# Moving the last mLSTM head ahead of the last attention pair, and splitting the branch sums into eight parts beside the gate units

## The chip, the cores and the metric

The kernel runs on one core of a Trainium2 chip. A core has five engines that run in parallel, each through its own instruction stream in a fixed order: TensorE (PE, matrix products), VectorE (DVE), ScalarE (ACT), GpSimd (POOL) and SyncE (SP, which here issues nearly all DMAs). An instruction that waits holds up everything behind it on its engine. The metric is the device time of one execution, in microseconds (us); lower is better.

## The reference

One decoder layer on x of 1024 tokens by 1024 channels, in float32. A combined projection feeds two branches: a 4-head mLSTM and a dilated attention with three head groups, whose outputs are summed with weights from their softmax denominators. Both are gated and merged; a SwiGLU block follows. Cut to what matters here:

```python
h    = rmsnorm(x, norm_mix_g)
proj = h @ w_in                       # q,k,v,i,f,o of the mLSTM; q,k,v of attention; two gates
hm   = mlstm_cell(q_m, k_m, v_m, ig, lf)             # 4 heads, chunk by chunk
y_a  = sigmoid(o_pre) * groupnorm(hm)
for g in range(3):                                   # dilations 1, 4, 16
    o_g, lse_g = dilated_window_attention(q_a[g], k_a[g], v_a[g], ...)
wts  = softmax(stack(lses), axis=0)                  # weight of each group, per token and head
y_b  = sum(wts[..., None] * stack(outs), axis=0)     # the sums this change moves
merged = sigmoid(g_A) * (y_a @ w_proj_a) + sigmoid(g_B) * (y_b @ w_proj_b)
x    = x + merged @ w_out
x    = x + (silu(hf @ w_gate) * (hf @ w_up)) @ w_down     # hf = rmsnorm(x)
out  = rmsnorm(x, norm_final_g)
```

## The kernel before

Every product is made in three matmuls on split operands (high and low parts, `whi`/`wlo` for weights), accumulated in PSUM. The projections of 256 columns (a "unit") go through `gemm_s`: a scheme of seven block products of 12 matmuls each (P1, P7, P6, P5, P2, P4, P3; 84 matmuls of 128x512 in all), with three PSUM banks of tag `mm`. ACT copies a first bank out (`u`), DVE adds bank and copy (line 299), and four evacuations follow. For a gate unit an evacuation is the DVE add of line 735, a tanh on ACT, and a store to `gt_d`. A unit's weights come as two raw pieces (tag `raw`, 128x4x256, two buffers), are combined on DVE (lines 244 to 247) and split on ACT and POOL (lines 106, 107).

The steps of the middle of the kernel stand in the string `ORDER`: `mH` is mLSTM head H (two units for q and k, the unit of its output gate, then `mlstm_core`, a chain of small steps), `aGP` an attention pair (two units, then `attn_core`), `rG` moves the maxima and denominators of group G to rows in DRAM (`ml_d`), `c` is `attn_combine`, which makes the group weights and stores them in `c_d` (line 703), `gN` is gate unit N (0 to 3 and 8 to 11; 4 to 7 are the output gates inside the heads), and `sI` the sums of output rows I. A sum multiplies each group's numerators (`num_d`) by its weights, broadcast from `c_d` over 64 partitions by two half loads, and adds the three products (lines 718 and 720); the result is stored in `yb_d`. One 128x512 piece of it needs three pairs of tiles of tag `c`, of which there are six buffers, shared with `mlstm_core`, `attn_core` and the loads behind. `merge_b` (from line 1033 on) loads `yb_d`, splits it into tiles of tag `t`, and multiplies by `w_proj_b` (lines 187 to 189). It needs all of `yb_d` for each of its outputs.

The order within each engine is not the order of the code: a scheduler places instructions by their modelled readiness, with code order as priority and some steps raised by `tc.high_priority()`. Buffers are given out in code order. What results on each engine is fixed before the kernel runs.

Of the kernel before, what the change touches and what calls it, by code (L numbers as in the profile page):

```python
# [14 lines left out]
ALU = mybir.AluOpType  # L15
# [4 lines left out]
P = 128  # L20
S = 1024
# [19 lines left out]
def layer_kernel(ctx, tc, x, norm_mix_g, w_in, b_gate_if, conv_w, conv_b, mlstm_norm_g,  # L41
# [3 lines left out]
    ACT, DVE, POOL, PE, SP = nc.scalar, nc.vector, nc.gpsimd, nc.tensor, nc.sync  # L45
# [10 lines left out]
    def T(tag, shape, dt=F32):  # L56
        cnt[0] += 1
        return sb.tile(list(shape), dt, tag=tag, bufs=SBT[tag], name=f"{tag}{cnt[0]}")
# [223 lines left out]
    def gemm_s(src, c0, B, evac, bk=("mm",) * 4, u1=None):  # L282

        front = u1 is not None
        ops = w7(src, c0, ("A11", "A12") if front else ())
        ba, bc, u2, u3 = PS(bk[0]), PS(bk[1]), T("u", (P, 512)), T("u", (P, 512))
        if not front:
            run_s(ops, "P1", B, ba, True)
            u1 = T("u", (P, 512))
            with tc.high_priority():  # L290
                ACT.activation(u1, ba, AF.Copy)
        run_s(ops, "P7", B, bc, True)
        run_s(ops, "P6", B, ba, front)
        with tc.high_priority():
            if front:
                DVE.tensor_tensor(u2, u1, ba, op=ALU.add)
            else:
                ACT.activation(u2, ba, AF.Copy)  # L298
            DVE.tensor_tensor(u3, u2, bc, op=ALU.add)  # L299
        bd = PS(bk[2])  # L300
        run_s(ops, "P5", B, bd, True)
        evac(1, 1, bd, u3)
        if not front:
            bx = PS(bk[3])
            run_s(ops, "P2", B, bx, True)
            evac(0, 0, bx, u1)
        run_s(ops, "P4", B, bc, False)
        evac(1, 0, bc, u2)
        run_s(ops, "P3", B, bd, False)
        evac(0, 1, bd, u2)  # L310
# [64 lines left out]
    nums_d = [[dr.tile([P, S], F32, name=f"num_d{g}{i}", tag=f"num_d{g}{i}") for i in range(4)] for g in range(3)]  # L375
# [328 lines left out]

    yb_d = [dr.tile([P, S], F32, name=f"yb_d{i}", tag=f"yb_d{i}") for i in range(4)]

    def attn_sum(i):
        for n in range(2):
            sl = slice(n * 512, (n + 1) * 512)
            acc = None  # L710
            for g in range(3):
                cb, nu = T("c", (P, 512)), T("c", (P, 512))
                base = c_d[g, 2 * i]
                for a in range(2):
                    SP.dma_start(cb[a * 64:(a + 1) * 64, :],
                                 bass.AP(tensor=base.tensor, offset=base.offset + a * S + n * 512, ap=[[0, 64], [1, 512]]))
                SP.dma_start(nu, nums_d[g][i][:, sl])
                DVE.tensor_tensor(nu, cb, nu, op=ALU.mult)
                if g:
                    DVE.tensor_tensor(acc, acc, nu, op=ALU.add)  # L720
                else:
                    acc = nu
            SP.dma_start(yb_d[i][:, sl], acc)


    gt_d = dr.tile([24, P, S], F32, name="gt_d", tag="gt_d")
# [4 lines left out]
    def gate_evac(i0):  # L731
        def ev(m, n, p, add):
            t_ = T("e", (P, 512))
            with tc.high_priority():
                DVE.tensor_tensor(t_, p, add, op=ALU.add)
                ACT.activation(t_, t_, AF.Tanh, scale=0.5)
                SP.dma_start(gt_d[i0 + m, :, n * 512:(n + 1) * 512], t_)
        return ev

    def load_gate(tag, i, n):  # L740
        t_ = T(tag, (P, 512))
        SP.dma_start(t_, gt_d[i, :, n * 512:(n + 1) * 512])
        return t_
# [235 lines left out]
        ACT.activation(hi, t1s[k], AF.Copy)  # L979
        DVE.tensor_tensor(lo, t1s[k], f(hi), op=ALU.subtract)  # L980

    ORDER = "m0 a00 a01 r0 m1 a10 a11 r1 m2 a20 a21 r2 c m3 g0 s0 g1 s1 g2 s2 g3 s3 g8 g9 g10 g11".split()
    mlstm_gates()
    mlstm_v2(0)
    for g in range(3):
# [1 line left out]
    bias_rows()  # L987


    def gate_unit(i):  # L990
        i0, c0 = gate_units[i]
        gemm_s(w_in, c0, Bq, gate_evac(i0))

    nm, ll = ([C(f"{n_}{g}", (P, NT, 8)) for g in range(3)] for n_ in ("nm", "ll"))

# [6 lines left out]
    def mlstm_head(h):  # L1002
# [2 lines left out]
        gate_unit(4 + h)  # L1005
        mlstm_core(h, qd, kd)

    for step in ORDER:
        if step[0] == "a":
            attn_pair(int(step[1]), int(step[2]))  # L1010
        elif step[0] == "r":
            attn_rows(int(step[1]), nm[int(step[1])], ll[int(step[1])])
        elif step[0] == "m":
            mlstm_head(int(step[1]))
        elif step[0] == "c":
            attn_combine()
        elif step[0] == "s":
            attn_sum(int(step[1]))
        else:
            gate_unit(int(step[1:]))  # L1020


    mB_d = dr.tile([KD, P, S], F32, name="mB_d", tag="mB_d")
# [10 lines left out]
    def merge_b():  # L1034
        ybs = load_split(yb_d, "t")
        qa = forms_a()
        for u in range(4):
            def ev_z(m, n, p):
                t_ = load_gate("s" if m == 0 else "pt", G_B + 2 * u + m, n)
                DVE.scalar_tensor_tensor(t_, t_, 1.0, p, op0=ALU.add, op1=ALU.mult)  # L1040
                SP.dma_start(mB_d[2 * u + m, :, n * 512:(n + 1) * 512], t_)
            gemm_w(w_proj_b, 0, 4, u * 256, ybs, ev_z)
        return qa
# [96 lines left out]
    for half in range(2):  # L1140
        ts = range(4 * half, 4 * half + 4)
        for u in range(4):
            def ev(t, p):
                sl = slice(u * 256, (u + 1) * 256)
                DVE.scalar_tensor_tensor(acc[t][:, sl], p, 0.5, acc[t][:, sl], op0=ALU.mult, op1=ALU.add)
# [293 lines left out]
```

## Time and profile before

| | us |
|---|---|
| three runs: median (lowest to highest) | 2104.31 (2101.97 to 2121.0) |
| the profiled execution | 2114.06 |
| its span, first to last instruction | 2112.3 |
| TensorE busy within the span | 2016.4 (95%) |
| DVE, POOL, ACT busy | 1316.4, 958.0, 804.4 |

Times within the profile are counted from the start of the span. The mean granted TensorE clock is 0.981 of full speed. The profiled execution is 9.8 us above the median, so a change in it is carried over to the median as a difference.

### The profile page before, as it was taken

Reading aid. Unit: us, or ns where it says so; the run is one execution under the profiler, and the core shown is the slowest. Engines: PE = TensorE matmul, PEld = TensorE weight load, DVE = VectorE, ACT = ScalarE, POOL = GpSimd, SP = SyncE. Lnnn points to the kernel's source line nnn. Section 1 sums busy time; section 2 is a strip of 40 time slices with the busy share of each in tenths; the row PEclk is TensorE's granted clock in tenths of the full one; section 3 lists DMA queues with packets and bytes.
Section 4 is the critical chain, followed back from the end, with each engine's and each line's share of the span. In section 5 each row is a group of like instructions: output and inputs, shape, how many; then the busy total and the mean of one; then the engine's idle time right before and its main releaser. Section 6 shows DMA issues by size and latency. Waiting matters only on the chain.

```text
span 2112.3 us, 31530 instructions
## 1 busy us (share of the span) xinstructions
PE 2016.4 (95%) x11433; PEld 1686.7 (80%) x11433; DVE 1316.4 (62%) x2341; ACT 804.4 (38%) x1722; POOL 958.0 (45%) x723
## 2 busy tenths in 40 slices
PE   6999998999999999999988899999999999999998
PEld 6999877877777677777876677997788888889996
DVE  7832347666786677667757584437755645576776
ACT  5322243343443344345433332445233333344422
POOL 4444443321332224333434656455554555568870
PEclk9999999999999999999999899999999999999999
DMA  4243344433344435555459876753433333375422
GB/s 154 83 120 111 83 133 124 129 127 128 119 130 140 129 123 141 130 183 150 135 168 282 267 233 215 248 181 120 130 96 99 110 95 100 117 247 158 146 83 80
DMA packets 264486, 303.49 MB, mean 144 GB/s; under 512 B 51353, under 2 KB 187052, under 8 KB 264332
## 3 DMA queue, kind: packets, MB, share of 16 engines
q1 hardware_dynamic: 263036, 299.26, 45.8%
q10 hardware_dynamic: 1296, 2.23, 0.3%
q8 instruction: 90, 1.47, 0.3%
q14 instruction: 64, 0.52, 0.1%
HBM read 207.35 MB, written 94.08 MB: 143 GB/s over the span
## 4 chain that ended last, share of the span: by engine, by line
PE 48%; DMA 9%; DVE 8%; POOL 3%; issue 2%; ACT 2%; SPq 1%; DVEq 0%; POOLq 0%; ACTq 0%
PE pmm L268 7%; PE pmm L267 7%; PE pmm L266 7%; DMA c<-num_d 2%; PE pS L268 2%; PE pS L267 2%; PE pS L266 2%; DMA raw<-in_w_in 2%; POOL wlo L107 2%; PE pmm L210 1%; PE pmm L209 1%; PE pmm L211 1%; PE pmm L1314 1%; PE pmm L1315 1%; PE pS L562 1%
## 5 line engine op out<-in xcount | busy, mean ns | idle before, releaser
L107 POOL TENSOR_TENSOR wlo<-sm,whi 128x512 fp32r<-128x512 f32 (+1 forms) x260 | 366.1, 1419 | 512.7 <-ACT whi L106 478.3
L107 POOL TENSOR_TENSOR wlo<-raw,whi 128x512 fp32r<-128x512 f32 (+3 forms) x228 | 339.5, 1502 | 393.5 <-ACT whi L106 376.2
L266 PE MATMUL pmm<-h,whi 128*128 128x512 f32 x824 | 334.1, 405 | 16.8 <-ACT u L298 13.2
L268 PE MATMUL pmm<-h,wlo 128*128 128x512 f32 x824 | 332.1, 403 | 3.8 <-POOL wlo L107 3.8
L267 PE MATMUL pmm<-h,whi 128*128 128x512 f32 x824 | 331.7, 403 | 0.0
L106 ACT ACTIVATE whi<-sm 128x512 fp32r<-128x512 f32 (+1 forms) x260 | 158.8, 634 | 263.2 <-PE pmm L267 128.5
L106 ACT ACTIVATE whi<-raw 128x512 fp32r<-128x512 f32 (+3 forms) x228 | 146.4, 669 | 217.9 <-issue 62.3
L266 PE MATMUL pmm<-t,whi 128*128 128x512 f32 x504 | 204.9, 407 | 13.6 <-DVE u L299 10.5
L266 PEld LDWEIGHTS pmm<-h,whi 128*128 128x128 f32 x824 | 158.5, 192 | 62.4 <-ACT u L298 16.6
L268 PE MATMUL pmm<-t,wlo 128*128 128x512 f32 x504 | 204.0, 405 | 0.0
L267 PE MATMUL pmm<-t,whi 128*128 128x512 f32 x504 | 204.0, 405 | 0.0
L268 PEld LDWEIGHTS pmm<-h,wlo 128*128 128x128 f32 x824 | 157.1, 191 | 41.6 <-POOL wlo L107 4.9
L267 PEld LDWEIGHTS pmm<-h,whi 128*128 128x128 f32 x824 | 157.4, 191 | 38.3 <-issue 3.6
L244 DVE TENSOR_TENSOR sm<-raw,raw 128x512 f32<-128x512 f32 x58 | 44.9, 774 | 181.0 <-DMA raw<-in_w_gate 61.7
L266 PEld LDWEIGHTS pmm<-t,whi 128*128 128x128 f32 x504 | 97.3, 193 | 39.1 <-DVE u L299 12.7
L849 DVE SCALAR_TENSOR_TENSOR c<-c,pm__329,c 128x256 f32<-128x256 f32 x192 | 111.3, 624 | 20.8 <-ACT c L847 20.0
L268 PEld LDWEIGHTS pmm<-t,wlo 128*128 128x128 f32 x504 | 96.7, 192 | 22.9 <-issue 2.2
L267 PEld LDWEIGHTS pmm<-t,whi 128*128 128x128 f32 x504 | 96.6, 192 | 22.3 <-issue 1.5
L589 ACT ACTIVATE s<-s,nm 128x256 f32<-128x256 f32 (+1 forms) x128 | 59.6, 467 | 83.8 <-DVE nm L584 52.3
L209 PE MATMUL pmm<-whi,h 128*128 128x256 f32 (+1 forms) x224 | 64.7, 295 | 5.2 <-DVE ifp L398 4.3
L211 PE MATMUL pmm<-whi,h 128*128 128x256 f32 (+1 forms) x224 | 64.1, 297 | 5.4 <-DVE h L163 3.3
L298 ACT ACTIVATE u<-pmm 128x512 f32<-128x512 f32 x54 | 31.9, 590 | 91.7 <-PE pmm L268 91.7
(549 smaller groups left out, 5065.9 us busy)
## 6 DMA issues: line engine op xcount, KB each, us to landing
raw<-in_w_in SPq DMA_DIRECT2D x74, 512.0 KB
gt_d<-e SPq DMA_DIRECT2D x48, 256.0 KB
raw<-in_w_gate SPq DMA_DIRECT2D x24, 512.0 KB
raw<-in_w_up SPq DMA_DIRECT2D x24, 512.0 KB
raw<-in_w_out SPq DMA_DIRECT2D x16, 512.0 KB
va_d<-u SPq DMA_DIRECT2D x24, 256.0 KB
s<-gt_d SPq DMA_DIRECT2D x24, 256.0 KB
qa_d<-e SPq DMA_DIRECT2D x24, 256.0 KB
```

The source lines that it names most:

```text
L106: ACT.activation(dh, src, AF.Copy)
L107: POOL.tensor_tensor(dl, src, f(dh), op=ALU.subtract)
L209: PE.matmul(p, sh, wh, start=(k == 0), stop=False)
L210: PE.matmul(p, sh, wl, start=False, stop=False)
L211: PE.matmul(p, sl, wh, start=False, stop=(k == K - 1))
L244: DVE.tensor_tensor(s1, a21, a22, op=ALU.add)
L266: PE.matmul(bank, wh[:, k, :], bh, start=start and k == 0, stop=False, skip_group_check=True)
L267: PE.matmul(bank, wh[:, k, :], bl, start=False, stop=False, skip_group_check=True)
L268: PE.matmul(bank, wl[:, k, :], bh, start=False, stop=k == 3, skip_group_check=True)
L298: ACT.activation(u2, ba, AF.Copy)
L589: ACT.activation(s[:, o:o + w], s[:, o:o + w], AF.Exp, bias=nm[:, qt, c:c + 1], accum_out=ll[:, qt, c:c + 1])
L849: DVE.scalar_tensor_tensor(y[:, m, :], xr[:, m, j:j + 256], cw[:, kt, j:j + 1], y[:, m, :], op0=ALU.mult, op1=ALU.add)
```

## The change

`ORDER` puts `m3` (the last mLSTM head) between the units of the attention pairs `a20` and `a21`, so that the pair `a21` is now the last step before `r2` and `c`. The steps `s0` to `s3` go; their work is cut into eight parts (output rows i, token half n), which are attached to the gate units g1 (1 part), g2 (1), g3 (2), g8 (2) and g9 (2). `gate_unit` issues the loads of its first part ahead of its products; after every second evacuation it emits the part's multiplies and adds behind that evacuation on DVE (`tc.issue_after`), and then the loads of the next part. Besides, `merge_b` now writes the four gate loads of a unit ahead of the unit's products instead of in each evacuation.

```diff
+    def sum_load(i, n):
+        sl, tiles = slice(n * 512, (n + 1) * 512), []
+        for g in range(3):
+            cb, nu = T("c", (P, 512)), T("c", (P, 512))
+            base = c_d[g, 2 * i]
+            for a in range(2):
+                SP.dma_start(cb[a * 64:(a + 1) * 64, :],
+                             bass.AP(tensor=base.tensor, offset=base.offset + a * S + n * 512, ap=[[0, 64], [1, 512]]))
+            SP.dma_start(nu, nums_d[g][i][:, sl])
+            tiles.append((cb, nu))
+        return tiles
+
+    def sum_add(i, n, tiles):
+        acc = tiles[0][1]
+        for g, (cb, nu) in enumerate(tiles):
+            DVE.tensor_tensor(nu, cb, nu, op=ALU.mult)
+            if g:
+                DVE.tensor_tensor(acc, acc, nu, op=ALU.add)
+        SP.dma_start(yb_d[i][:, n * 512:(n + 1) * 512], acc)
...
-    ORDER = "m0 a00 a01 r0 m1 a10 a11 r1 m2 a20 a21 r2 c m3 g0 s0 g1 s1 g2 s2 g3 s3 g8 g9 g10 g11".split()
+    ORDER = "m0 a00 a01 r0 m1 a10 a11 r1 m2 a20 m3 a21 r2 c g0 g1 g2 g3 g8 g9 g10 g11".split()
...
-    def gate_unit(i):
+    def gate_unit(i, part=None):
         i0, c0 = gate_units[i]
-        gemm_s(w_in, c0, Bq, gate_evac(i0))
+        base, parts, calls = gate_evac(i0), list(part or ()), [0]
+        tiles = [sum_load(*parts[0])] if parts else []
+
+        def ev(m, n, p, add):
+            ins = base(m, n, p, add)
+            calls[0] += 1
+            if parts and calls[0] % 2 == 0:
+                with tc.issue_after(getattr(ins, "ins", ins)):
+                    sum_add(*parts.pop(0), tiles.pop())
+                if parts:
+                    tiles.append(sum_load(*parts[0]))
+        gemm_s(w_in, c0, Bq, ev)
...
-        elif step[0] == "s":
-            attn_sum(int(step[1]))
         else:
-            gate_unit(int(step[1:]))
+            n = dict(g1=1, g2=1, g3=2, g8=2, g9=2).get(step, 0)
+            gate_unit(int(step[1:]), [divmod(npart + j, 2) for j in range(n)])
+            npart += n
...
         for u in range(4):
+            gts = {(m, n): load_gate("s" if m == 0 else "pt", G_B + 2 * u + m, n) for m in range(2) for n in range(2)}
+
             def ev_z(m, n, p):
-                t_ = load_gate("s" if m == 0 else "pt", G_B + 2 * u + m, n)
+                t_ = gts[m, n]
```

The new `m3` stands ahead of `a21` in code order, so its core gets the `c` buffers first and the core of `a21` comes behind it. Three places show what stands where. In the rows a tile's name carries its counter and a serial number behind the underscore.

On DVE, before, the first multiply of a sum (L718 on `c1691`) stands among the last steps of the last mLSTM head's core (L852, L916) and the weight sums of gate unit 9 (L245 to L247), while gate unit 8 is on TensorE:

```order
L852 SCALAR_TENSOR_TENSOR c1655_9794<-s1656_9804,c1655_9794 128x512
L245 TENSOR_TENSOR sm1832_10772<-sm1832_10772,raw1830_10768 128x512
L916 SCALAR_TENSOR_TENSOR s1660_9822<-c1655_9794,s1659_9819 128x256 x2
L718 TENSOR_TENSOR c1691_10033<-c1690_10032,c1691_10033 128x512
L246 TENSOR_TENSOR sm1833_10773<-raw1830_10768 128x512
L247 TENSOR_TENSOR sm1833_10773<-raw1831_10770,sm1832_10772 128x512
```

Now the same multiply (L723) stands behind the combine step (L695 to L702) and behind all four evacuations (L738) of gate unit 9:

```order
L738 TENSOR_TENSOR e1842_10830<-pmm1841_10817,u1839_10776 128x512
L698 TENSOR_TENSOR cmb1_9875<-cmb0_9874,cmb1_9875 128x192
L699 TENSOR_TENSOR pt1666_9877<-cmb1_9875 128x64
L700 TENSOR_TENSOR pt1666_9877<-pt1666_9877,cmb1_9875 128x64
L701 RECIPROCAL pt1666_9877<-pt1666_9877 128x64
L702 TENSOR_TENSOR cmb0_9874<-cmb0_9874,pt1666_9877 128x192
L738 TENSOR_TENSOR e1844_10847<-pmm1843_10834,u1840_10789 128x512
L738 TENSOR_TENSOR e1851_10884<-pmm1837_10774,u1838_10775 128x512
L738 TENSOR_TENSOR e1852_10900<-pmm1841_10817,u1838_10775 128x512
L723 TENSOR_TENSOR c1691_10033<-c1690_10032,c1691_10033 128x512
L723 TENSOR_TENSOR c1693_10038<-c1692_10037,c1693_10038 128x512
L725 TENSOR_TENSOR c1691_10033<-c1691_10033,c1693_10038 128x512
```

So the 40 multiplies and adds moved from beside gate units 8 to 11 to beside gate units 10 and 11 and behind them.

On DVE at the last evacuations, before, the last add of a sum (L720 on `c1802`) stands ahead of the last three evacuations (L735) of gate unit 11, the last unit ahead of `merge_b`, whose side begins at L1102:

```order
L299 TENSOR_TENSOR u1891_11087<-u1890_11086,pmm1889_11085 128x512
L718 TENSOR_TENSOR c1806_10619<-c1805_10618,c1806_10619 128x512
L735 TENSOR_TENSOR e1894_11141<-pmm1893_11128,u1891_11087 128x512
L720 TENSOR_TENSOR c1802_10606<-c1802_10606,c1806_10619 128x512
L735 TENSOR_TENSOR e1896_11158<-pmm1895_11145,u1892_11100 128x512
L735 TENSOR_TENSOR e1897_11174<-pmm1889_11085,u1890_11086 128x512
L735 TENSOR_TENSOR e1898_11190<-pmm1893_11128,u1890_11086 128x512
L1102 TENSOR_TENSOR c1939_11268<-c1937_11260,c1936_11258 128x512
```

Now the last evacuation of that unit (L738 on `e1898`) stands there, with sums behind it:

```order
L738 TENSOR_TENSOR e1897_11174<-pmm1889_11085,u1890_11086 128x512
L723 TENSOR_TENSOR c1788_10553<-c1787_10552,c1788_10553 128x512
L738 TENSOR_TENSOR e1898_11190<-pmm1893_11128,u1890_11086 128x512
L725 TENSOR_TENSOR c1784_10543<-c1784_10543,c1788_10553 128x512
L723 TENSOR_TENSOR c1811_10674<-c1810_10673,c1811_10674 128x512
L723 TENSOR_TENSOR c1813_10679<-c1812_10678,c1813_10679 128x512
L725 TENSOR_TENSOR c1811_10674<-c1811_10674,c1813_10679 128x512
L723 TENSOR_TENSOR c1815_10684<-c1814_10683,c1815_10684 128x512
```

Sixteen of the 40 stand behind the last evacuation, nine of the 24 multiplies among them; before, none did.

On SP, before, the first loads of a sum (L715 from `c_d`, L717 from `num_d`) stand behind the gate stores (L737) of unit 3:

```order
L737 DMA gt_d_327<-e1793_10564 128x512
L737 DMA gt_d_327<-e1794_10580 128x512
L715 DMA c1690_10032<-c_d_310 64x512
L101 DMA raw1831_10770<-in_w_in 128x4x256
L715 DMA c1690_10032<-c_d_310 64x512
L717 DMA c1691_10033<-num_d00_297 128x512
```

Now the store of `c_d` itself (L703) stands behind a gate store of unit 9, and the first loads (L714, L716) behind two more:

```order
L740 DMA gt_d_327<-e1842_10830 128x512
L101 DMA raw1876_11052<-in_w_in 128x4x256
L703 DMA c_d_310<-cmb0_9874 128x3x64
L746 DMA pt1958_11350<-gt_d_327 128x512
L740 DMA gt_d_327<-e1844_10847 128x512
L714 DMA c1690_10032<-c_d_310 64x512 x2
L740 DMA gt_d_327<-e1851_10884 128x512
L716 DMA c1691_10033<-num_d00_297 128x512
L714 DMA c1692_10037<-c_d_310 64x512 x2
L716 DMA c1693_10038<-num_d10_301 128x512
```

All 72 loads of the sums moved behind the gate store of unit 9's second evacuation; among and behind them on the queue, as far as the last load, stand ten gate stores and four weight pieces of 128x4x256.

## Rows read from the trace of the kernel before

**Rows 1.** The page: span, and busy time of each engine.
```profile
span 2112.3 us, 31530 instructions
PE 2016.4 (95%) x11433; PEld 1686.7 (80%) x11433; DVE 1316.4 (62%) x2341; ACT 804.4 (38%) x1722; POOL 958.0 (45%) x723
```

**Rows 2.** Windows: stretch, length, busy and count by engine, clock, DMA share, GB/s.
```profile
core 0: us, PE busy (x) PEld busy (x) DVE busy (x) ACT busy (x) POOL busy (x), PEclk, DMA share, GB/s
...
1090.00:1138.20 48.20, 36.84 (x145) 28.29 (x144) 31.64 (x62) 12.86 (x24) 15.36 (x12) 0.93 0.85 260
1138.20:1157.90 19.70, 19.24 (x83) 15.01 (x82) 13.57 (x19) 6.80 (x12) 8.72 (x7) 1.00 0.90 287
1157.90:1184.00 26.10, 21.78 (x83) 16.95 (x82) 12.92 (x16) 9.34 (x17) 12.60 (x11) 0.87 0.80 252
```

**Rows 3.** Waits in total, 1060 to 1200 us: us, times, longest.
```profile
DVE c L718 <- DMA c<-num_d: 24.8, 14, 5.9
...
PE pmm L187 <- DVE s L1040: 3.0, 1, 3.0
```

**Rows 4.** TensorE in order of time: start, us, [idle before, releaser].
```profile
1109.47 0.76 PE L266 MATMUL pmm<-t,whi 128*128 128x512 f32 x1 [2.76 <-DVE e L735]
...
1176.12 0.80 PE L266 MATMUL pmm<-t,whi 128*128 128x512 f32 x1 [4.11 <-DVE u L299]
...
1184.08 0.39 PE L187 MATMUL pmm<-t,whi 128*128 128x512 f32 x1
```

**Rows 5.** The SP queue in order of time, 1000 to 1180 us.
```profile
1006.80 0.36 SPq L703 DMA_DIRECT2D c_d<-cmb  x1
...
1076.44 0.48 SPq L715 DMA_DIRECT2D c<-c_d  x1
...
1123.13 0.32 SPq L723 DMA_DIRECT2D yb_d<-c  x1
...
1172.95 0.33 SPq L717 DMA_DIRECT2D c<-num_d  x1
...
1178.84 0.32 SPq L723 DMA_DIRECT2D yb_d<-c  x1
```

**Rows 6.** DVE in order of time, the last multiplies and the last add.
```profile
1172.23 0.69 DVE L718 TENSOR_TENSOR c<-c,c 128x512 f32<-128x512 f32 x1 [5.89 <-DMA c<-num_d]
...
1175.38 0.68 DVE L299 TENSOR_TENSOR u<-u,pmm 128x512 f32<-128x512 f32 x1
1175.98 0.68 DVE L718 TENSOR_TENSOR c<-c,c 128x512 f32<-128x512 f32 x1
...
1177.19 1.62 DVE L720 TENSOR_TENSOR c<-c,c 128x512 f32<-128x512 f32 x1
```

**Rows 7.** The chain that ended last, in order of time: start, us, what.
```profile
1087.87 5.93 DMA c<-num_d
```

**Rows 8.** DMA issued in 1076 to 1182 us: count, KB each.
```profile
DMA packets 16419, 26.22 MB, mean 247 GB/s; under 512 B 1859, under 2 KB 5443, under 8 KB 16412
...
c<-c_d SPq DMA_DIRECT2D x48, 128.0 KB
c<-num_d SPq DMA_DIRECT2D x24, 256.0 KB
gt_d<-e SPq DMA_DIRECT2D x15, 256.0 KB
...
yb_d<-c SPq DMA_DIRECT2D x8, 256.0 KB
```

**Rows 9.** The window with the fastest DMA near the change.
```profile
1210.00:1220.00 10.00, 10.00 (x44) 8.13 (x43) 7.62 (x9) 3.46 (x6) 3.84 (x4) 1.00 1.05 390
```

**Rows 10.** POOL, 1170 to 1215 us: the split of the loaded sums, x8.
```profile
L107 POOL TENSOR_TENSOR t<-c,t 128x512 fp32r<-128x512 f32 x8 | 10.3, 1301 | 6.7 <-ACT t L106 6.7
```

**Rows 11.** Around the combine before: a window, and TensorE's transposes.
```profile
970.00:1000.00 30.00, 27.50 (x204) 20.95 (x194) 23.07 (x46) 14.06 (x31) 11.80 (x11) 0.94 0.45 136
...
985.13 1.13 PE L677 MATMUL pS<-cs,ll 128*8 128x128 f32 x8 [2.02 <-DVE s L684]
```

More of the change, by code (lines that the diff above doesn't have):

```diff
@@ L705, in layer_kernel @@
     yb_d = [dr.tile([P, S], F32, name=f"yb_d{i}", tag=f"yb_d{i}") for i in range(4)]
[L707 to L723, printed above, removed]
+    def sum_load(i, n):
[16 more added lines that the diff above has]
+        SP.dma_start(yb_d[i][:, n * 512:(n + 1) * 512], acc)
     gt_d = dr.tile([24, P, S], F32, name="gt_d", tag="gt_d")
@@ L734, in ev @@
             with tc.high_priority():
-                DVE.tensor_tensor(t_, p, add, op=ALU.add)
+                ins = DVE.tensor_tensor(t_, p, add, op=ALU.add)
                 ACT.activation(t_, t_, AF.Tanh, scale=0.5)
                 SP.dma_start(gt_d[i0 + m, :, n * 512:(n + 1) * 512], t_)
+            return ins
         return ev
@@ L1006, in mlstm_head @@
         mlstm_core(h, qd, kd)
+    npart = 0
     for step in ORDER:
```

## The prediction

> **What bounds the kernel now.** I read the page first: TensorE is busy for 95% of the span [rows 1], so an edit pays only where TensorE stands still or runs at a low clock, and costs only where it makes a new gap. Next the windows around the sums. The boundaries are put where one gate unit ends: 83 matmuls are recorded (of 84) in 1138.2 to 1157.9, unit 10, and 83 in 1157.9 to 1184.0, unit 11 [rows 2]. Undisturbed, a matmul takes 19.24/83 = 0.232 us, so a unit takes 19.5 us. From 1090 to 1138.2 (units 8 and 9) TensorE is busy 36.8 of 48.2 us at a clock of 0.93; unit 10 is nearly clean; unit 11 takes 26.1 us.
>
> What ends these gaps is seen in order of time: TensorE waits 2.76 us for an evacuation (DVE L735) and 4.11 us for a bank addition (DVE L299) [rows 4]. DVE is not slow there, it stands: its multiplies L718 wait 24.8 us in 14 places for the numerator load [rows 3], and L299 at 1175.38 comes right behind such a multiply, which had waited 5.89 us [rows 6]. A load issued at 1087.87 takes 5.93 us [rows 7]; the DMA engines are 80 to 90% taken at 252 to 287 GB/s [rows 2]. So from 1087 to 1179 the binding chain is load, multiply, add, freed buffer, next load. The first product of `merge_b` follows at 1184.08 with no wait of its own [rows 4].
>
> **What the change removes.** Up to the end of gate unit 9 the sums are gone from DVE and SP. The idle time of 1090 to 1138.2 goes, 48.2 - 36.84 = 11.4 us, and the lost clock, 0.07 x 48.2 = 3.4 us: 14.8 us. All of it is counted as the sums' doing. The work on TensorE up to that point is otherwise the same: both orders then have the last head, the last pair and six gate units behind them. So unit 9 ends at 1138.2 - 14.8 = 1123.4.
>
> **What it moves.** The weights of the sums come from `c_d`. Before, that was written at 1006.80 and the first load followed at 1076.44, held up by the `c` buffers [rows 5]. The new order writes it between the first and the second evacuation of unit 9, and the first numerator load stands behind the gate store of the third. The third evacuation has one product of 12 matmuls (2.8 us) behind it and needs the add and the tanh (1.4 us, an estimate: two steps of 128x512 at the 0.69 us of [rows 6]), so that load goes out about 1 us before the unit ends. Its latency lies between 3.0 us (the load at 1172.95, multiplied at 1175.98) and 5.9 us [rows 5 to 7]: the first multiply runs 2 to 5 us after the end of unit 9, and I take 3.5.
>
> Then 23 more pairs of tiles. Two paces can be read. *With gate units beside*: the third to the eighth store of `yb_d` stand at 1123.13 and 1178.84 [rows 5], (1178.84 - 1123.13)/5 = 11.1 us for three pairs, 3.7 us a pair. The new order has much the same traffic beside the sums while units 10 and 11 run: ten gate stores and four weight pieces in 39 us, 4.7 MB, against 1.2 MB in each 11.1 us before (what 275 GB/s leave beside 1.8 MB of sums). So 10 pairs take 37 us, and TensorE, which needs 2 x 19.5 = 39 us for the two units, is hardly held up: the last bank addition (u1891) stands behind 10 to 11 pairs on DVE. *Alone*: a pair is 512 KB, and a third of a 256-KB store, 0.61 MB [rows 8], 2.1 us at 287 GB/s. With six buffers, of which one holds the running sum, 2.5 pairs are in flight; 3.0 us of latency, two DVE steps of 0.69 us and about 1 us of issue make 5.4/2.5 = 2.2 us. I take 2.3, so the other 13 pairs take 30 us.
>
> The last add is done at 1123.4 + 3.5 + 37 + 30 = 1193.9; before it was at 1177.19 + 1.62 = 1178.8 [rows 6]. What follows: before, the first product came 5.3 us later, behind the tail of unit 11. Now unit 11 is long done, and the first pieces of `yb_d` can be loaded and split ahead of the last add; but all eight pass POOL at 1.3 us each, 10.4 us [rows 10], and the last one goes through a store and a load. I take 3 us (bounds 0 and 8). `merge_b` starts at 1196.9 instead of 1184.1: **12.8 us later**. TensorE should then stand still from about 1163, the end of unit 11, to 1197.
>
> The rest at nothing: the order of the matmuls behind `merge_b`'s start is the same; the earlier gate loads are hidden by the queue, and at best take away the 3.0 us that a product of `merge_b` waited for its bank [rows 3]. DVE has the same 40 steps. The interchange of head and pair is free as long as TensorE finds gate units to run beside the small chains, as it does before.
>
> The sum against the profiled execution is 2114.1 + 12.8 = 2126.9 us, and against the median, which lies 9.8 us below it, 2104.3 + 12.8 = **2117 us**. A measurement of this kernel tells about 1% (21 us) from no change, so this is most likely a small loss within that bound.
>
> **Bounds of the pace.** All that has to move behind unit 9's end is 12.6 MB of loads, 2.1 MB of sums and 4.7 MB beside them, 19.4 MB. The fastest window near by moves 390 GB/s [rows 9]: 50 us, so the last add is at 1123.4 + 3.5 + 50 = 1176.9, `merge_b` at 1180, 4 us *earlier* than before. If all 23 pairs go at 3.7 us, it is 1123.4 + 3.5 + 85 + 3 = 1215, 31 us later.
>
> In the Trainium skill, "DMA: Bandwidth & Descriptors", section Rules for kernel authors, the advice on overlap is to issue a DMA early, compute, and wait late. It speaks for this change, which puts each part's loads ahead of a unit's products. Here the loads can't go early, since `c_d` is not there. The same page's Bandwidth table has 341 GB/s for a 1 MB transfer; by that estimate the 19.4 MB take 57 us and `merge_b` starts at 1187, 3 us later than before. The rows of this place show 252 to 287 GB/s, and the measurement decides.
>
> **Rivals.**
>
> *The sums keep the loaded pace.* With few buffers the pace may be set by the ring and the latency under load, not by the bytes; then it is 3.7 us to the end. For it: a load of 5.9 us in the chain [rows 7] while the DMA share was only 0.8 to 0.9 [rows 2]. Against: behind unit 11 nothing else is on the queues. Price +31 us: 2135.
>
> *The sums run at the fast rate and fit.* Without the mLSTM core's traffic and with DVE free of its small steps, the DMA engines reach the 390 GB/s of [rows 9]. Then `merge_b` starts 4 us earlier: 2100, not slower. It decides from a pace of about 2.1 us a pair *with* the units beside (20 us for 10 pairs and so on), against 3.7 now. A gain over 1% would need all 23 pairs within the 39 us of units 10 and 11, that is 1.7 us a pair, beside 4.7 MB more.
>
> *The pair's tail comes late.* The last attention core, its transposes for `r2` and the combine now follow the head's core, and stand in TensorE's fixed order beside units 3, 8 and 9. Where they are not ready, TensorE stands and `c_d` comes later. Before, this stretch cost 2.5 us of idle time in 970 to 1000, 2.02 of them at the transposes L677, at a clock of 0.94 [rows 11]. Had it three times that, unit 9 ends 8 to 9 us later and everything behind it too: +22 us, 2126.
>
> **How the numbers follow.** The forecast, with its own spread of 2107 to 2127, has 0.50; the loaded pace 0.20; the fast rate 0.20; the late tail 0.10. The range of 2099 to 2137 takes in the rivals and leaves out 0.1 on each side. Faster by over 1% (below 2083) is only the far end of the fast rate: 0.05. Slower by over 1% (above 2125) is most of the loaded pace, half of the late tail and a tenth of the forecast: 0.17 + 0.05 + 0.06 + a little for what I have missed, 0.30. Within 1%: 0.65.
>
> **What would show it.** In the profile of the changed kernel: units 8 and 9 without gaps, and no wait for DVE L299 or L738 there; `c_d` written about 5 us before the end of unit 9; the first multiply L723 behind that unit's end; 10 or 11 pairs done when unit 11 ends; one gap of some 33 us on TensorE ahead of `merge_b`, at whose end stands the split of the sums, followed by a few microseconds at the lower clock; loads faster in that gap than beside the units. It would be wrong if the gap is under 20 us (the pace of the sums was DVE's queue, not the loads), if units 10 and 11 are stretched, or if gaps open around the last attention core.

## The result and the profile after

| | before | after |
|---|---|---|
| median, us (10 runs each) | 2105.21 | 2124.73 |
| range of the runs, us | 2101.57 to 2121.0 | 2120.8 to 2128.78 |
| profiled execution, span, us | 2112.3 [rows 1] | 2123.2 |

The change makes the kernel slower: ratio 1.0083, 95% interval 1.0066 to 1.0099, some 17 us. The prediction of 2117 us lies 8 us under the median; its range of 2099 to 2137 us holds the measured time.

The page of the changed kernel, span and engines, answers to [rows 1]; the work of TensorE is the same, the span is longer.

```profile
span 2123.2 us, 31534 instructions
PE 2009.1 (95%) x11433; PEld 1681.3 (79%) x11433; DVE 1318.0 (62%) x2341; ACT 805.4 (38%) x1722; POOL 959.4 (45%) x723
```

The windows, cut at the end of unit 9, within unit 10 (1140) and at the end of unit 11, answer to [rows 2]:

```profile
core 0: us, PE busy (x) PEld busy (x) DVE busy (x) ACT busy (x) POOL busy (x), PEclk, DMA share, GB/s
1090.00:1120.50 30.50, 30.50 (x199) 23.89 (x198) 18.59 (x37) 13.10 (x35) 11.99 (x10) 1.00 0.61 192
1120.50:1140.00 19.50, 13.90 (x58) 10.70 (x57) 10.94 (x15) 3.61 (x6) 6.20 (x5) 0.95 0.77 226
1140.00:1168.60 28.60, 27.64 (x108) 21.33 (x106) 16.47 (x21) 8.83 (x15) 9.94 (x7) 0.92 0.86 267
1168.60:1200.80 32.20, 0.00 (x0) 0.00 (x0) 14.03 (x21) 2.41 (x4) 1.62 (x1) 0.55 0.77 238
```

Up to 1120.5 TensorE has no gap; from 1120.5 to 1168.6 it runs units 10 and 11 (166 of 168 matmuls recorded); then it does nothing for 32.2 us. What it waited for stands in order of time, as in [rows 4]:

```profile
1139.23 0.80 PE L266 MATMUL pmm<-t,whi 128*128 128x512 f32 x1 [5.37 <-DVE u L299]
...
1200.82 0.79 PE L187 MATMUL pmm<-t,whi 128*128 128x512 f32 x1 [32.25 <-ACT t L106]
...
1215.66 0.50 PE L187 MATMUL pmm<-t,whi 128*128 128x512 f32 x1 [3.93 <-DVE s L1060]
```

The middle row is the first matmul of `merge_b`, which stood at 1184.08 before. Its releaser is the split (L106) of the first loaded sum. The queue that loads go through, as in [rows 5]:

```profile
1115.55 0.37 SPq L703 DMA_DIRECT2D c_d<-cmb  x1
1118.84 1.12 SPq L714 DMA_DIRECT2D c<-c_d  x2
1120.64 0.45 SPq L716 DMA_DIRECT2D c<-num_d  x1
...
1135.73 0.33 SPq L726 DMA_DIRECT2D yb_d<-c  x1
...
1171.24 0.39 SPq L101 DMA_DIRECT2D raw<-in_w_proj_b  x1
1171.68 0.56 SPq L716 DMA_DIRECT2D c<-num_d  x1
...
1173.51 0.54 SPq L740 DMA_DIRECT2D gt_d<-e  x1
...
1194.78 0.43 SPq L716 DMA_DIRECT2D c<-num_d  x1
1195.81 4.82 SPq L1048 DMA_DIRECT2D c<-yb_d  x4
1201.04 0.32 SPq L726 DMA_DIRECT2D yb_d<-c  x1
```

The weights are stored at 1115.55, not at 1006.80; the first numerator load goes out at 1120.64; the eight parts leave between 1135.73 and 1201.04, 65.3/7 = 9.3 us apart. The rows at 1194.78 and 1195.81 show how the gap ends: the first loads of finished sums (L1048) stand on SP behind the last numerator load, although the first of those sums was stored at 1135.73. VectorE in order of time, as in [rows 6]:

```profile
1126.33 1.90 DVE L723 TENSOR_TENSOR c<-c,c 128x512 f32<-128x512 f32 x2 [5.10 <-DMA c<-num_d]
...
1136.23 2.35 DVE L723 TENSOR_TENSOR c<-c,c 128x512 f32<-128x512 f32 x2
1138.50 0.68 DVE L299 TENSOR_TENSOR u<-u,pmm 128x512 f32<-128x512 f32 x1
...
1171.20 0.69 DVE L723 TENSOR_TENSOR c<-c,c 128x512 f32<-128x512 f32 x1 [1.07 <-DMA c<-num_d]
...
1178.97 0.69 DVE L723 TENSOR_TENSOR c<-c,c 128x512 f32<-128x512 f32 x1 [5.41 <-DMA c<-num_d]
...
1199.59 0.69 DVE L723 TENSOR_TENSOR c<-c,c 128x512 f32<-128x512 f32 x1 [0.33 <-DMA c<-num_d]
1200.32 0.69 DVE L725 TENSOR_TENSOR c<-c,c 128x512 f32<-128x512 f32 x1
```

Fourteen multiplies are done when unit 11 ends, ten come behind it. From the first to the last they take 73.3 us for 23 pairs, 3.2 us each, and the ten behind unit 11 are on average no faster: 1171.20 to 1199.59 is 28.4 us for nine pairs, 3.2 us. That average has two parts. The first of the nine takes 7.8 us, to 1178.97: its numerator load (1171.68) goes out between a 512-KB weight piece for `merge_b` and the last gate store, and the DMA engines are 87% taken at 269 GB/s from 1168.6 to 1179. The other eight take 20.6 us, 2.6 us each, at 72% and 222 GB/s from 1179 to 1200. So the traffic of the units reaches some 5 us past unit 11's end on TensorE, and only behind it do the sums run alone. The row at 1138.50 is the one that TensorE waited 5.37 us for: a bank addition that stands behind an add, two multiplies and three weight sums of unit 11 (L245 to L247, whose raw piece VectorE had waited 3.25 us for). In the waits in total of 1120 to 1202 us, as in [rows 3], the numerator load leads for DVE as it did before (24.8 us there), and a new name has come: the split of the sums' loads.

```profile
PE pmm L187 <- ACT t L106: 32.5, 2, 32.3
...
DVE c L723 <- DMA c<-num_d: 30.5, 16, 5.4
```

One table serves all runs below, each with its ratio to the kernel before on the same chip. It holds the starts of three stages on TensorE in the profiled executions (the first matmuls of `merge_b`, of the merge over the heads, of the output product), and what is left to the end of the span.

| run | `merge_b` | heads' merge | output | rest | median | ratio to before, 95% |
|---|---|---|---|---|---|---|
| before | 1184.1 | 1236.1 | 1322.2 | 790.1 | | |
| after | 1200.8 | 1254.2 | 1337.5 | 785.7 | 2124.73 | 1.0083 (1.0066 to 1.0099) |
| order_alone | 1200.5 | 1255.2 | 1338.3 | 795.2 | 2123.06 | 1.0111 (1.0074 to 1.0148) |
| parts_old_order | 1176.3 | 1229.5 | 1315.1 | 788.0 | 2102.98 | 1.0007 (0.9991 to 1.0022) |
| standin | 1186.3 | 1238.9 | 1322.1 | 789.5 | 2114.43 | 1.0048 (1.0031 to 1.0064) |
| half_bytes | 1188.2 | 1241.1 | 1324.0 | 788.0 | 2112.56 | 1.0046 (1.0028 to 1.0063) |
| wide_ring | 1186.2 | 1234.9 | 1318.3 | 791.0 | 2112.22 | 1.0043 (1.0029 to 1.0058) |
| standin_wide | 1172.5 | 1226.9 | 1315.0 | 788.6 | 2103.96 | 1.0013 (1.0001 to 1.0025) |
| late_parts | 1181.8 | 1231.8 | 1315.3 | 783.9 | 2099.41 | 0.9997 (0.9979 to 1.0014) |
| late_wide | 1168.2 | 1223.0 | 1308.0 | 788.8 | 2100.76 | 0.9991 (0.9977 to 1.0006) |
| early_parts2 | 1164.5 | 1230.6 | 1314.2 | 789.5 | 2105.88 | 1.0024 (1.0003 to 1.0045) |
| early_wide | 1156.1 | 1221.7 | 1305.5 | 792.1 | 2097.09 | 0.9980 (0.9967 to 0.9992) |
| pair_first_wide | 1192.0 | 1242.9 | 1329.2 | 789.9 | 2117.19 | 1.0070 (1.0055 to 1.0086) |
| split_core | 1189.1 | 1248.5 | 1332.8 | 787.2 | 2120.54 | 1.0068 (1.0044 to 1.0092) |

The rest varies by 11 us between executions with no pattern in it, so the ratio judges the time, and the stages say where. One of the seven executions of `split_core` took 3529.04 us at a granted clock of 0.768; its ratio leaves that one out, its median does not.

### The profile page after: what moved, and what is told of

The parts are those of the page before. It is cut to its first block, busy times and chain, and to the rows that moved or that the text cites. A ratio compares the mean times of both kernels' runs of the same rounds, so it can differ in the third digit from the quotient of the medians.

```text
span 2123.2 us, 31534 instructions
## 1 busy us (share of the span) xinstructions
PE 2009.1 (95%) x11433; PEld 1681.3 (79%) x11433; DVE 1318.0 (62%) x2341; ACT 805.4 (38%) x1722; POOL 959.4 (45%) x723
## 5 line engine op out<-in xcount | busy, mean ns | idle before, releaser
L106 ACT ACTIVATE whi<-sm 128x512 fp32r<-128x512 f32 (+1 forms) x260 | 158.9, 634 | 262.8 <-PE pmm L267 133.5
L106 ACT ACTIVATE whi<-raw 128x512 fp32r<-128x512 f32 (+3 forms) x228 | 146.3, 669 | 214.6 <-issue 65.4
L266 PE MATMUL pmm<-t,whi 128*128 128x512 f32 x504 | 202.1, 401 | 7.9 <-DVE u L299 7.9
L267 PE MATMUL pmm<-t,whi 128*128 128x512 f32 x504 | 202.2, 401 | 0.0
```

The costliest lines, as they stand in the source:

```text
L106: ACT.activation(dh, src, AF.Copy)
L266: PE.matmul(bank, wh[:, k, :], bh, start=start and k == 0, stop=False, skip_group_check=True)
L267: PE.matmul(bank, wh[:, k, :], bl, start=False, stop=False, skip_group_check=True)
```

## The experiments

### Which part of the change acts

`order_alone` is the kernel before with one line changed; `parts_old_order` is the changed kernel with that line put back.

```diff
-    ORDER = "... m2 a20 a21 r2 c m3 g0 s0 g1 s1 g2 s2 g3 s3 g8 ..."
+    ORDER = "... m2 a20 m3 a21 r2 c g0 s0 g1 s1 g2 s2 g3 s3 g8 ..."
```

> The kernel before with the new order of steps only: the last head ahead of the last pair, the sums whole and written behind units 0 to 3 as they were, no early gate loads. Theory A (the order makes the weights late, and nothing else in the change acts): as the whole change, 2124 us, 1.006 to 1.010 of before, weights stored at about 1115, a gap of 30 to 34 us on TensorE ahead of the second merge product's first matmul. Rival B (the eight parts and their queueing behind evacuations make the loss, or a share of it): 2105 to 2115, and the gap under 20 us.

> The kernel before with everything but the new order: eight parts, queued behind evacuations of units 1 to 9, and the early gate loads. Theory A: no difference from before, 2105 us within 0.3%, the first load of the weights at about 1076 as before, because the buffers of the last head's core hold it back and the evacuations that the parts stand behind are long past by then. Rival B: the parts change the time, by up to 15 us either way.

The order alone gives 2123.06 us, and its first matmul of `merge_b` reads as the changed kernel's:

```profile
1200.50 0.79 PE L187 MATMUL pmm<-t,whi 128*128 128x512 f32 x1 [31.63 <-ACT t L106]
```

The rest of the change with the old order gives 2102.98 us, not to be told from before. Built, `order_alone` has the same instructions in the same order on every engine as the changed kernel, and `parts_old_order` the same as the kernel before, buffer numbers apart. The eight parts, their edges to evacuations of units 1 to 9 and the early gate loads change no row of the program: those evacuations are long past when the weights and the buffers come, so the edges never bind. Theory A holds and B is out. Since `parts_old_order` is the kernel before executed once more, it also shows the spread of one program: its `merge_b` starts at 1176.3, the profiled execution of before at 1184.1.

### Why the sums come late

`standin` takes the weights' loads from `nm_d`, written hundreds of us earlier.

```diff
-            base = c_d[g, 2 * i]
+            base = nm_d[2 * i % 4]
```

> The changed kernel, but the sums' weights are read from a tensor that is written hundreds of us earlier, in the same shape and as many loads; the weighting of the heads is left out. Theory A (the whole loss is that the weights come at 1115): the sums start when the last attention core has left the buffers, at about 1085 to 1090, 24 pairs at 3.2 us take 77 us, the last add is at about 1165, the gap on TensorE shrinks from 32 to under 10 us, 2095 to 2105 us. Rival F (the interchange of head and pair costs something else as well): above 2112.

Theory A's number did not come out: 2114.43 us, in the range of rival F. F's cause does not follow from that, since the rows show another one at work, a slower pace. The sums do start early, but the last one leaves no earlier than this:

```profile
1087.26 0.38 SPq L717 DMA_DIRECT2D c<-num_d  x1
...
1185.96 0.32 SPq L727 DMA_DIRECT2D yb_d<-c  x1
```

98.7 us for 24 pairs is 4.1 us each, beside units and the rest of the pair's core; between the same two rows the changed kernel takes 80.4 us, 3.4 us each. The weights' lateness is about half of the loss; the other half is the pace, which the next two runs take up. `half_bytes` loads 256 of 512 columns in every load of the sums, and stores the summed half twice. `wide_ring` leaves the loads and gives the numerators buffers of other sets that are idle here, so that the six buffers hold weights alone.

```diff
-            cb, nu = T("c", (P, 512)), T("c", (P, 512))
+            cb, nu = T("c", (P, 512)), T("st" if g == 0 else "s", (P, 512))
```

> The changed kernel with every load of the sums cut to half its columns, as many loads, buffers, steps and waits; half of each sum is left out, and the stored half is stored twice. Theory G (the bytes set the pace of the sums): alone 3.0 us a pair becomes 1.5 to 1.8, the last add comes at 1165 to 1170, the gap is under 10 us, 2098 to 2104 us. Rival H (latency and the six buffers set it): 2.5 us a pair or more, the last add at about 1188, 2112 to 2118 us.

> The changed kernel with the numerators of the sums in two other sets of buffers (two and three of them, idle at that time), so that the six buffers hold weights alone and twice as many pairs are under way. Theory G (bytes): the same pace and time, 2120 to 2127 us. Rival H (the ring): 2.0 us a pair, the last add at 1175 to 1180, 2103 to 2110 us.

Half the bytes: 2112.56 us, a last store at 1187.52 and a gap of 24 us are rival H's numbers. The parts leave between 1132.15 and 1187.52, 7.9 us apart, 2.6 us a pair instead of 3.1, measured between stores. Where the sums run alone, from the first to the second of these rows, seven pairs take 2.0 us each, against 2.6 for the last seven of the changed kernel:

```profile
1172.37 0.42 DVE L723 TENSOR_TENSOR c<-c,c 128x256 f32<-128x256 f32 x1 [5.25 <-DMA c<-num_d]
...
1186.61 0.42 DVE L723 TENSOR_TENSOR c<-c,c 128x256 f32<-128x256 f32 x1 [0.92 <-DMA c<-num_d]
```

The sixteen multiplies ahead of them, beside the units, lie 2.75 us apart instead of 3.2. So in both places halving the bytes takes away a quarter of a pair's time or less, and bytes are its smaller share. They act through the latency too: from issue to multiply the last nine numerator loads take 2.8 us on average, against 4.9 us with all the bytes.

The wide ring fell between its theories, at 2112.22 us. SP's queue shows what it did.

```profile
1048.04 0.43 SPq L716 DMA_DIRECT2D st<-num_d  x1
1053.15 0.55 SPq L716 DMA_DIRECT2D st<-num_d  x1
...
1126.55 0.33 SPq L726 DMA_DIRECT2D yb_d<-st  x1
...
1185.85 0.38 SPq L726 DMA_DIRECT2D yb_d<-st  x1
```

Five numerators are loaded ahead of the first weights (1116.49), two of them by over 60 us, and the first part leaves 9.2 us earlier; the parts then lie 8.5 us apart instead of 9.3. The DMA engines are now nearly full (share 0.97, the column before last), so bytes are the likely limit; the wide ring with half the bytes was not run:

```profile
1160.00:1180.00 20.00, 4.72 (x21) 3.47 (x19) 11.87 (x16) 3.46 (x6) 2.55 (x2) 0.68 0.97 285
```

So neither rival wins outright: with six buffers the ring and the load's latency, which itself falls with the bytes, hold the pace at about 3.1 us a pair, and with more of them it is 2.8.

`standin_wide` puts the two cures together; it too leaves the weighting out.

> The changed kernel with the early stand-in for the weights (the weighting of the heads is left out) and the numerators in the other buffers as well. Theory I (lateness of the weights and the six buffers together make the whole loss, each about half): 2098 to 2104 us, the last add at about 1165, the gap ahead of the merge under 5 us. Rival J (both runs shortened the same stretch, or the interchange of head and pair costs something of its own): 2108 us or more.

2103.96 us, ratio 1.0013: theory I in the time, though the last store leaves at 1179.37, so its last add is later than 1165. In `merge_b`'s start the cures gain 14.5 us (weights), 14.6 us (ring) and 28.3 us together, so they add. Against the kernel before, late weights and a ring with no room for numerators make up the loss to within 0.3%. That does not show the interchange of head and pair to be free: the kernel before has the narrow ring too. Against the old order with the wide ring (`late_wide` below) `standin_wide` starts `merge_b` 4.3 us and the output product 7.0 us later, so a cost of a few microseconds stays open.

### Could the gaps of the kernel before be taken away?

The prediction counted 14.8 us of gain in units 8 and 9. `late_parts` tries to have it without the loss: the old order, the parts moved to units 8 to 11, where the edges do bind. VectorE's order now has three multiplies behind every second evacuation.

```diff
-            n = dict(g1=1, g2=1, g3=2, g8=2, g9=2).get(step, 0)
+            n = dict(g8=2, g9=2, g10=2, g11=2).get(step, 0)
```

> The old order of steps, but the parts stand beside units 8 to 11, two each, so that the edge to an evacuation binds: each part's three multiplies come behind the second or fourth evacuation of a unit, not ahead of it. Theory C (the idle time of units 8, 9 and 11 came from evacuations that stood behind multiplies waiting for their loads): the units run at 19.5 us, unit 11 ends at about 1163 instead of 1184, the last add at 1167, the merge starts at 1172: 12 us earlier than before, 2093 us. Rival D (the loads' pace decides, 11.1 us for a part against 9.75 us for half a unit): 8 x 11.1 = 89 us from 1095, the merge starts at 1187 to 1190, 2108 to 2111 us, and evacuations wait behind the multiplies of the part ahead.

Theory C's time falls, and so does rival D's: 2099.41 us, ratio 0.9997. Unit 11 ends at 1170 and the merge then waits for the last part, whose numerator is late again:

```profile
1178.64 0.69 DVE L723 TENSOR_TENSOR c<-c,c 128x512 f32<-128x512 f32 x1 [5.86 <-DMA c<-num_d]
```

```profile
1181.78 0.80 PE L187 MATMUL pmm<-t,whi 128*128 128x512 f32 x1 [11.38 <-ACT t L106]
```

The gaps beside the units and the wait ahead of the merge read as one quantity, the pace of the sums (3.8 us a pair here, 3.8 and 3.9 in `parts_old_order` and before, from the first multiply to the last), shown in two places. `late_wide` adds the other buffers to this:

> The old order with the parts beside units 8 to 11 and the numerators in the other buffers, so that a part's loads can go out while the part ahead is summed. Rival H (the ring): a part is ready when its evacuation is, units 8 to 11 lose under 5 us, the last add follows unit 11's end at about 1165, the merge starts at 1172, 2088 to 2094 us. Theory G (bytes): as with the six buffers, 2098 to 2102 us, the last add at about 1180.

The merge starts at 1168.2, with a wait of 1.15 us, 8 us ahead of the same old order in `parts_old_order`, as rival H said; but the ratio of 0.9991 shows no gain, and 2100.76 us is theory G's time. Against that run the lead is 8.1 us at `merge_b` and 7.1 us at the output product, and the ratio's interval ends at 0.9977, 5 us. These runs don't settle how much of the difference is the spread of executions.

`early_parts2` goes the other way: the sums ahead of the last head's core, beside units 1, 2, 3 and 8 (`k3` is the core).

```diff
-    ORDER = "... a20 m3 a21 r2 c g0 g1 g2 g3 g8 g9 g10 g11"
+    ORDER = "... a20 a21 r2 c m3 g0 g1 g2 g3 g8 k3 g9 g10 g11"
```

> Attention pair and combine first as in the kernel before, then the last head's products and gate unit, then units 0 to 3 and 8, and only then the last head's core; the parts stand beside units 1, 2, 3 and 8, two each, behind second and fourth evacuations. The weights are there at about 1007, the buffers too, since the head's core now comes behind the sums. Theory A with C: units 9 to 11 have no sums beside them, the last add comes at about 1125, and the 21 us of idle time and low clock of units 8, 9 and 11 go: 2084 us. Rival D (pace 3.7 us a pair, 11.1 us for a part against half a unit of 9.75): 1.4 us of idle time for each of 7 parts, 2094 us. Rival E (the core, moved back, is late for the merge over the heads or holds up units 9 to 11): 2105 us or more, with waits for its results in the merge.

2105.88 us, rival E. The merge starts at 1164.5, 12 us ahead of `parts_old_order`, and then takes 66.2 us instead of 53.2. The core's last rows are stored at 1199.99, well behind the start of `merge_b`, beside which the operands of the heads' merge are made from them. `early_wide` adds the other buffers:

> Pair, combine and the last head's products ahead of the sums, its core behind them, as before, but with the numerators in the other buffers, so that the parts are shorter and the core starts earlier than when it had to store its last rows at 1199.99, behind the merge's start. Theory K (that lateness alone, 66 us for the second merge product instead of 53, kept this order from gaining): the core is done by 1165, the merge starts at about 1160 and takes 53 us, 2088 to 2094 us. Rival E (two stretches of small work on VectorE cannot be moved without holding evacuations elsewhere): 2098 us or more.

2097.09 us, ratio 0.9980: 4 us faster than before, the only version whose interval lies below both kernels, and less than theory K wanted. Its condition, a core done by 1165, was not reached: the last rows are stored at 1191.37. The merge starts at 1156.1 and takes 65.6 us, again long. VectorE at that place, in order of time:

```profile
1167.94 1.27 DVE L935 SCALAR_TENSOR_TENSOR l_den<-l_den 128x4 f32<-128x4 f32 x1
...
1169.24 1.22 DVE L936 TENSOR_TENSOR l_den<-l_den,g_em 128x4 f32<-128x4 f32 x1
1170.50 0.18 DVE L937 RECIPROCAL l_r<-l_den 128x4 f32<-128x4 f32 x1
...
1175.42 1.18 DVE L119 TENSOR_TENSOR rq_tl<-rq_sl 128x4 f32<-128x4 f32 x1
1176.64 0.16 DVE L120 SCALAR_TENSOR_TENSOR rq_tl<-rq_tl,l_t 128x4 f32<-128x4 f32 x1
...
1178.09 0.69 DVE L1064 SCALAR_TENSOR_TENSOR s<-s,pmm 128x512 f32<-128x512 f32 x1
```

The last row frees a bank that TensorE waits 6.36 us for; it stands behind the last core's small steps. The next two runs try to bring that core forward. `pair_first_wide` has the last pair and the combine ahead of the third head as well; `split_core` puts the core's first half ahead of the sums.

```diff
-    ORDER = "... m2 a20 a21 r2 c m3 g0 g1 g2 g3 g8 k3 g9 ..."
+    ORDER = "... a20 a21 r2 c m2 k2 m3 g0 g1 g2 g3 k3 g8 g9 ..."    pair_first_wide
+    ORDER = "... m2 a20 a21 r2 c m3 k3 g0 g1 g2 g3 g8 k3 g9 ..."    split_core
```

> The last attention pair, its rows and the combine ahead of both the third and the last head, the sums behind the third head's core beside the last head's gate unit and units 0 to 2, the last core behind them, numerators in the other buffers. Theory K: the weights come some 50 us before the sums want them, the last core is done by 1150, nothing is late for the merge, 2084 to 2092 us. Rival C (in this order the multiplies stand ahead of evacuations on VectorE again): the gaps of 10 to 15 us come back beside units 0 to 2, 2098 to 2103 us.

> The last head's core in two: its first half ahead of the sums, its second half behind them, beside units 8 to 10; otherwise as the run with the core whole behind the sums and the numerators in the other buffers, in which that core's last rows were stored at 1191 and the second merge product took 66 us, with its bank additions behind the core's small steps on VectorE. Theory K: with the core's last rows stored by 1160, the merge product takes 53 us again; it starts at about 1160, 2088 to 2093 us. Rival E (what is taken from the end is lost beside the sums, where multiplies now stand between the evacuations of units 1 to 8): the merge starts at 1168 or later, 2096 us or more.

Both are slower than before, by 0.70% and 0.68%, and theory K fails in both. In `pair_first_wide` evacuations and bank additions stand behind multiplies again while the sums run (TensorE's waits, 980 to 1080 us):

```profile
PE pmm L266 <- DVE e L739: 5.8, 2, 3.1
PE pmm L266 <- DVE u L299: 4.8, 2, 4.2
```

These 10.6 us are the gaps of rival C, but the time of 2117.19 us is 14 us beyond its range. In 700 to 1192 us the transposes of the heads' cores (L952) wait 7.4 us besides, against 0.5 us before; what makes the rest stays open.

`split_core` is rival E's, with `merge_b` at 1189.1. TensorE waits likewise, 1050 to 1160 us, and the core's last rows are stored at 1213.09, later than ever, since the parts lie 13.6 us apart (1055.15 to 1150.07) with half a core beside them:

```profile
PE pmm L266 <- DVE u L299: 13.5, 3, 5.3
```

## Why the prediction came out, step by step

*The gaps of units 8 and 9 go.* Right: 30.50 of 30.50 us busy from 1090 to unit 9's end, at 1120.5 where 1123.4 was said. Counting all of the idle time as the sums' doing was not quite right: in the trace of before TensorE waits there 1.83 us for L120 and 0.53 us for L941, steps of the last head's core, which the new order moves away as well. Nor does L299 at 1175.38 come right behind the multiply that had waited 5.89 us: a second multiply, with a wait of 1.13 us, and an add stand between.

*`c_d` some 5 us before the end of unit 9, the first multiply 3.5 us behind it.* The store at 1115.55 is 4.95 us ahead of the end. The multiply at 1126.33 comes 5.8 us behind it, beyond the 2 to 5 given: the load waited for was issued at 1120.64, on the unit's end and not 1 us before it, and its multiply came 5.7 us later, inside the 3.0 to 5.9 given for the latency.

*10 pairs at 3.7 us beside the units, TensorE hardly held up.* The pace was 3.2 us, and 14 pairs were multiplied by unit 11's end. But TensorE was held up: 48.1 us for two units instead of 39, 5.37 of it at one bank addition, and a granted clock of 0.92 to 0.95 (between its two levels of 1.2 and 2.4 GHz) besides. The prediction names stretched units as a sign that it would be wrong, and this sign came. By these rows it cost nothing, since the sums and not the units set the merge's start.

*13 pairs alone at 2.3 us.* This is the term that was mis-sized: the pairs behind unit 11 took 3.2 us each. The estimate took 3.0 us of latency, the shortest load that it had read, and 2.5 pairs under way. From issue to multiply the last nine numerator loads took 3.3 to 7.3 us, 4.9 on average; the fifteen before them took 5.0, so the loads were not faster in the gap, as the prediction wanted. With 4.9 in place of 3.0 its own sum gives (4.9 + 1.4 + 1)/2.5 = 2.9 us (an estimate). The rest is the 7.8 us of the first pair, beside traffic of the units that the prediction counted as over; the eight pairs behind it ran at 2.6 us, near the forecast. The rival of the loaded pace was right that the pace would on average stay, at 3.2 us and not its 3.7; once the other traffic was gone, the sums did go faster. In the sum: 67.0 us forecast from the first multiply to the end of the last add, 74.7 measured; with the start 0.6 us earlier than forecast, the last add ends at 1201.0, 7.1 us late.

*`merge_b` 3 us behind the last add.* It starts 0.2 us before its end, released by the first split sum, so 3.2 us of the 7.1 are made up here. The wait of 3.93 us at 1215.66 is no part of this: the same wait, for a bank that DVE's L1060 (L1040 before) frees behind steps that wait for loads of `ya_d`, was 3.0 us before [rows 3] and 4.53 us in `parts_old_order`. The gap of 32.25 us has the size forecast (33) by luck: it began some 6 us late, with the stretched units, and ended 4 us late, with the sums.

*12.8 us.* In the profiled executions `merge_b` moved by 16.7 us. The execution of before that I read had started it 7.8 us later than the next execution of the same program (`parts_old_order`); against that one it moved by 24.5 us, and the medians moved by 19.5. So 12.8 was low by 3.9 us, what the pace of the sums and the earlier start of `merge_b` leave, and by a base that was late in its own spread, as far as one execution of each tells. The prediction carried the 9.8 us between its profile and the median over as if they lay outside the stretch that changes; 7.8 us of them lay in or ahead of it.

*The rest at nothing.* The early gate loads and the eight parts: shown, the program's rows are the same without them. The early gate loads don't take away the wait of 3.0 us either, as said above. The tail of the pair: TensorE was busy 38.93 of 40 us in 1040 to 1080, and its waits from 1000 to 1121 come to 1.6 us; no stall of the kind feared in [rows 11].

The Trainium skill, "DMA: Bandwidth & Descriptors", section Rules for kernel authors, advises to issue a DMA early and wait late. `wide_ring` shows this at work where data allow it: numerators issued at 1048.04 and 1053.15 go with a first part that leaves 9.2 us earlier. The changed kernel could not follow it with numerators in the weights' ring.

## What to carry to other kernels

Before a producer is moved later to clear the place where its consumer disturbs, count what work is left for the consumer to hide behind: here 24 pairs at 3.2 us met two units of 19.5 us. Several small waits and one large wait can be the same quantity; in `late_parts` a cleaner order moved it and did not shrink it. What has to change is the pace itself (buffers, latency, bytes), and when that pace is estimated, the latency goes in as the loads of the place show it on average, not as the shortest one: 4.9 us here, not 3.0. Where a scheduler sets the order, compare the built orders first: of three edits in this change, two left no trace in the program.

## What the runs showed of the hardware

Most of VectorE's steps on 128x4 elements took 1.0 to 1.27 us from 1167.94 to 1175.42 in `early_wide`, and 0.16 us from 1176.64 on. GpSimd ran subtractions of 128x512 without a break in that time, 1.25 us each, the last one this:

```profile
1175.33 1.25 POOL L107 TENSOR_TENSOR wlo<-raw,whi 128x512 fp32r<-128x512 f32 x1
```

The steps of VectorE take about as long as GpSimd's instruction, and the last long one ends with it (1176.60 and 1176.58); the reciprocal among them, with one input, still took 0.18 us, but two steps with one tile in (`TENSOR_SCALAR`, L940 and L115) took 1.19 us. That the one waits for the other was read from these rows and not tried; it would explain why the last head's core, moved beside the splits of the merge, holds TensorE's banks so long. In the Trainium skill, "SBUF — State Buffer", section Who interferes with whom, a VectorE instruction with two SBUF inputs contends with a GpSimd instruction that reads SBUF. The rows of the steps with two inputs agree, and show the price for small steps: about 1.2 us in place of 0.16.

The granted clock after the 32 us gap, in the changed kernel:

```profile
1200.80:1205.00 4.20, 3.96 (x9) 2.78 (x10) 0.21 (x1) 1.89 (x3) 4.16 (x4) 0.50 0.90 291
1205.00:1210.00 5.00, 5.00 (x21) 4.04 (x20) 0.00 (x0) 3.45 (x7) 4.88 (x5) 0.88 0.81 266
```

It was 0.50 (1.2 GHz) from 1200.8 to 1205 and 0.88 on average from 1205 to 1210, so matmuls ran at the lower level for about 5 us after TensorE took up work again.
